# Token sums in spare operand tiles, and a feed-forward block whose down product runs beside its gate and up pairs

## The chip, the cores and the metric

One core of one Trainium2 chip runs the whole program in one launch. The metric is the device time of one execution in microseconds (us). Engines: PE (TensorE) multiplies, DVE (VectorE), ACT (ScalarE) and POOL (GpSimd) work elementwise, SP issues the loads.

## The reference, cut to what matters

Two blocks of two layers each work on x with 512 tokens and 1024 features. The change touches the feed-forward parts only:

```python
# first block, each layer
h = rms_norm(x, mlp_norm_w)
x = x + jnp.square(jax.nn.relu(h @ w_up)) @ w_down        # 4096 hidden features
# second block, each layer
def swiglu(h, w_gate, w_up, w_down):
    return (jax.nn.silu(h @ w_gate) * (h @ w_up)) @ w_down # 2816 hidden features
h = rmsnorm(x, ffn_pre_g[layer])
x = x + rmsnorm(swiglu(h, ffn_w_gate[layer], ffn_w_up[layer], ffn_w_down[layer]), ffn_post_g[layer])
```

The norms divide each token by its root mean square; the kernel applies that factor (`rb`, spread over partitions; `rT`, one column per block of 128 tokens) after the products, and only the per-feature weights before them.

## The kernel before, in words

All matrices lie with features on the partitions, so that a tile of 128 output features by 512 tokens is the sum of k products of a 128x128 weight block with a 128x512 input block. Every fp32 operand is split into a high part (fp32r, an ACT copy) and a low part (the difference, by DVE or POOL), and each block product is three matmuls: high by high, high by low, low by high (`mm3`, L318). `weights` (L260) loads one tile of weights into `raw` (4 buffers), and makes `whi` and `wlo` (3 buffers each). `fm_tiles` (L329) makes plain tiles: 8 blocks of inputs by 3 matmuls of 512 columns.

Most gate, up and hidden tiles are made in pairs by `seven` (L402), a Strassen-like scheme: seven half-size products (each 4 blocks by 3 matmuls of 256 columns, 84 matmuls in all) give two output tiles. It needs sums of weight quarters (`pair_weights`, L374: four POOL additions at L393 to L397 into two `sum` tiles, then an ACT copy to `shi` at L386 and a DVE subtraction to `slo` at L387) and sums of token halves (`token_sums`, L352, once for each feed-forward part: eight scaled ACT copies into the temporaries b1 and b2, sixteen DVE subtractions into four `sum` tiles one after the other, an ACT copy and a DVE subtraction into `tok`). `sum` has 2 buffers, which the token sums and the weight sums of the pairs share; b1 has 1 buffer and b2 is one of the four temporaries `t`. `shi` and `slo` have 3 buffers in the first block and 2 in the second.

`seven` is a generator with three steps: products 1 to 3 (p1 with the weight half a1, p2 and p3 with s12), then the second half of p1 and p2 with s34, then the last two (p2 with a2, p3 with s34) and `post`. In `mlp` (L948) and `swiglu` (L1344) `pairs` runs the first two steps of a pair and leaves the third to come after the first step of the next one (`finish`). The weight sums are issued in the first step.

In `mlp` four hidden tiles are plain (`up`), and after every 8 hidden tiles the down product of that group follows: 8 output tiles in a row (`down`, L971).

In `swiglu` tiles 0, 1 and 21 are plain (gate and up each), tiles 2 to 20 are 19 pairs. `post` multiplies gate and up by `rb` (L1364, L1365), takes silu on ACT (L1350) and the product on DVE (L1351), and splits the result: high part on ACT (L275), low part on POOL (L276). The hidden tiles fall into groups of 6, 6, 6 and 4; after each group its down product makes 8 output tiles in a row, copied to `m` by ACT for the first group (L1386) and added by DVE for the others (L1389). So five pairs stand in a row, then eight down tiles, and so on. `act`, the operand tiles of the hidden features, has 10 buffers in `mlp` and 8 in `swiglu`. `post_norm` (L1054) then norms `m` and adds it to x.

The order on each engine is made by the framework's planner from its own estimates of time, with the program's order as priority: an instruction written later can stand earlier on its engine. Each engine then works its list strictly in that order.

Of the kernel before, what the change touches and what calls it, by code (L numbers as in the profile page):

```python
# [8 lines left out]
F = mybir.dt.float32  # L9
R = mybir.dt.float32r  # L10
# [69 lines left out]
def host_arrays(inp):  # L80
# [69 lines left out]
    dn = g["ffn_w_down_2"]  # L150
    out["down012"] = np.stack([np.stack([fm(dn[l][768 * i:768 * i + 768]) for i in range(3)]) for l in range(2)])
    out["down3"] = np.stack([fm(dn[l][2304:]) for l in range(2)])
    out["odin"] = fm(g["od_w_in_2"][0])
# [7 lines left out]
class Net:  # L161
# [189 lines left out]

    def token_sums(self, x, g):  # L352


        nc, out, high = self.nc, [], self.last_high
        for k in range(4):
            b1, b2 = self.temp("b1", 1), self.temp()
            for i, b in enumerate((b1, b2)):
                nc.scalar.activation(b, x[k + 4 * i], AF.Copy, scale=g(k + 4 * i))
            (b11, b12), (b21, b22) = [(b[:, :256], b[:, 256:]) for b in (b1, b2)]  # L360
            f = self.get("sum", 2 * S)
            t1, t2, t3, t4 = [f[:, 256 * i:256 * i + 256] for i in range(4)]
# [39 lines left out]
    def seven(self, src, xg, tok, post):  # L402
# [18 lines left out]
        r, t, u = self.get("r", 256), self.temp(), self.temp()  # L421
        product(p1, a1, 0, plain(0, 0), True)
        product(p2, s12, 1, summed(1), True)
        product(p3, s12, 0, summed(0), True)
# [7 lines left out]
        nc.vector.tensor_add(u[:, half[1]], p3, u[:, half[1]])  # L432
        yield
        product(p2, a2, 0, summed(3), False)
        product(p3, s34, 1, plain(1, 1), False)
        nc.vector.tensor_add(u[:, half[0]], p2, r)
        nc.vector.tensor_add(t[:, half[1]], p3, t[:, half[1]])
        post(t, u)
# [59 lines left out]

    def mean_sq(self, accs, dim, eps=EPS, warm=False):


        nc = self.nc
        ps = self.av_tile()
        for i, acc in enumerate(accs):
            for tb in range(NB):
                self.stat_mm = nc.tensor.matmul(
                    ps[:, 2 * tb:2 * tb + 2], acc[:, tb * 128:(tb + 1) * 128], self.ones2,
                    start=i == 0 and tb == 0, stop=i == len(accs) - 1, skip_group_check=True)
            if warm:
                self.keep_warm(7, self.stat_mm)  # L510
        var = self.small(4, "var")
        nc.vector.tensor_scalar(var, ps[:, 0:8:2], 1.0 / dim, eps, op0=OP.mult, op1=OP.add)
        return var
# [434 lines left out]
    def mlp(self, l):  # L948
        nc, I, x = self.nc, self.I, self.x
        xg, _, rb = self.pre_norm("mlp_norm", l)  # L950
        acts = {}

# [24 lines left out]
        def pairs(js):  # L977
            for j in js:
                now = both(j)
                next(now)  # L980
                finish()
                next(now)
                left.append(now)

# [5 lines left out]
        up([3])  # L990
        tok = self.token_sums(x, lambda c: self.v("mlp_norm", 8 * l + c))
        pairs([4, 6])
# [60 lines left out]

    def post_norm(self, m, name, l, then, last=False):  # L1054

        nc = self.nc
        accs = self.sumsq(m, apart=True)
        rb = self.spread_psum(self.rsqrt(self.mean_sq(accs, 1024, warm=not last)))
        if not last:
# [17 lines left out]

    def post_pre_norm(self, m, post, pl, pre, l):
        xg = []

        def then(c):
            xg.append(self.split_scaled(self.x[c], self.v(pre, 8 * l + c), self.normed()))
            return self.last_low

        self.post_norm(m, post, pl, then)
        return (xg,) + self.rstd(self.sumsq(self.x, apart=True, eng=self.nc.gpsimd), 1024)
# [257 lines left out]
    def swiglu(self, l):  # L1344
        nc, I = self.nc, self.I
        xg, rT, rb = self.normed_x
        acts, m, left = {}, [], []

        def product(j, t, u):
            nc.scalar.activation(t, t, AF.Silu)  # L1350
            nc.vector.tensor_mul(t, t, u)  # L1351
            acts[j] = self.split(t, nc.gpsimd)

        def tile(ps):
            t = self.temp()
            nc.vector.tensor_mul(t, ps, rb)
            return t
# [4 lines left out]
        def both(j):  # L1362
            def post(t, u):
                nc.vector.tensor_mul(t, t, rb)  # L1364
                nc.vector.tensor_mul(u, u, rb)  # L1365
                product(j, t, u)
            return self.seven([I[n][l, j] for n in ("gate", "up")], xg, tok, post)

        def pairs(js):
            for j in js:  # L1370
                now = both(j)
                next(now)
                finish()
                next(now)
                left.append(now)

        def finish():
            while left:
                next(left.pop())

        def down(g, n, j):
            src = I["down012"][l, g, j] if g < 3 else I["down3"][l, j]
            ps = self.fm_tile(self.weights(src, n * 128, nc.vector), [acts[6 * g + k] for k in range(n)])
            if g == 0:
                t = self.get("m", S)
                nc.scalar.activation(t, ps, AF.Copy)  # L1386
                m.append(t)
            else:
                nc.vector.tensor_add(m[j], m[j], ps)  # L1389

        p = self.fm_tiles([plain("gate", 0), plain("up", 0), plain("gate", 1)], xg)
        last = self.fm_tiles([plain("up", 1)], xg)[0]
        tok = self.token_sums(self.x, lambda c: self.v("ffn_pre", 8 * l + c))
        product(0, tile(p[0]), tile(p[1]))
        product(1, tile(p[2]), tile(last))
        pairs(range(2, 6))
        for g, n in enumerate((6, 6, 6, 4)):
            if g < 3:
                pairs([6 * g + 6])
            down(g, n, 0)  # L1400
            finish()
            for j in range(1, 8):
                down(g, n, j)
            if g < 2:
                pairs(range(6 * g + 7, 6 * g + 12))
            elif g == 2:
                pairs([19, 20])
                t = tile(self.fm_tile(plain("gate", 21)[0], xg))
                finish()
                product(21, t, tile(self.fm_tile(plain("up", 21)[0], xg)))  # L1410
        if l == 0:
            self.normed_x = self.post_pre_norm(m, "ffn_post", 0, "mix_pre", 1)
        else:
            self.post_norm(m, "ffn_post", 1, self.store, last=True)

# [24 lines left out]
```

## Time and profile before

| what | value |
|---|---|
| three runs | 2532.81, 2529.24, 2529.79 us, median 2529.79 |
| the profiled execution | 2529.73 us, its span from first to last instruction 2528.0 us |
| PE busy | 2359.3 us (93%), DVE 1736.7 (69%), ACT 1216.2 (48%), POOL 1019.9 (40%) |
| mean granted TensorE clock | 0.978 |
| feed-forward parts | about 310 to 660 and 997 to 1305 us (first block), 1531 to 1907 and 2117 to 2528 us (second block) |

The profile is one execution. Lines such as L387 are lines of the kernel before. A row of the timeline is an instruction's start, its duration, its engine and line, what it writes and reads, and in brackets the idle time of the engine before it with the work that ended it. A matmul's duration overlaps its neighbours; the distance from start to start is what a matmul costs.

### The profile page before, as it was taken

To read this page: it belongs to the slowest core of one execution; us is meant where nothing else is said; L and a number is where in the kernel's file an instruction comes from. 1 tells how busy PE (TensorE), PEld (TensorE's weight loads), DVE (VectorE), ACT (ScalarE), POOL (GpSimd) and SP (SyncE) were. 2 spreads that over 40 slices of the span, in tenths; PEclk is the share of its full clock that TensorE was granted. 3 is DMA by queue.
4 is the path that set the end of the run, shared out by engine and by line. 5 is a ranking of instruction groups with operands and counts; after the bars stand their busy time and mean duration, and the time that the engine had idled before them with its cause. 6 is when DMAs were issued, how large, how long until landed. Compare 5 with 4: busy or idle time off the path is not lost.

```text
span 2528.0 us, 35109 instructions
## 1 busy us (share of the span) xinstructions
PE 2359.3 (93%) x13521; PEld 2028.6 (80%) x13521; DVE 1736.7 (69%) x2777; ACT 1216.2 (48%) x1945; POOL 1019.9 (40%) x691
## 2 busy tenths in 40 slices
PE   9999979999998998999999997999999989799997
PEld 7787778898877876898887875888986766788886
DVE  6978664665488886565558668856857676857765
ACT  5657653443365675443343474443434554444432
POOL 3465343343145642444312432553521542634531
PEclk9999989999999999999999999999999999899998
DMA  5311223333232111333332211333222321233231
GB/s 171 100 63 44 65 76 100 105 104 93 90 101 83 58 51 59 107 94 100 101 100 72 84 43 42 100 101 100 83 91 71 102 79 56 74 102 93 94 102 59
DMA packets 63850, 215.71 MB, mean 85 GB/s; under 512 B 7105, under 2 KB 7233, under 8 KB 63681
## 3 DMA queue, kind: packets, MB, share of 16 engines
q1 hardware_dynamic: 62064, 207.06, 26.9%
q0 software_dynamic: 1472, 6.29, 0.7%
q8 instruction: 106, 1.74, 0.3%
q14 instruction: 64, 0.52, 0.1%
q10 hardware_dynamic: 144, 0.11, 0.0%
HBM read 211.33 MB, written 2.10 MB: 84 GB/s over the span
## 4 chain that ended last, share of the span: by engine, by line
PE 69%; DVE 20%; ACT 4%; issue 4%; POOL 2%; DMA 0%; POOLq 0%; ACTq 0%; DVEq 0%
PE mm L323 19%; PE mm L322 19%; PE mm L321 19%; PE st L322 2%; PE st L321 2%; DVE wlo L387 2%; PE st L323 2%; DVE slo L387 1%; DVE x L1065 1%; DVE t L1365 1%; PE st L307 1%; DVE score L737 1%; DVE m L736 1%; PE st L308 1%; PE st L632 1%
## 5 line engine op out<-in xcount | busy, mean ns | idle before, releaser
L268 ACT ACTIVATE whi<-raw 128x1024 fp32r<-128x1024 f32 (+2 forms) x286 | 277.7, 973 | 488.5 <-PE mm L322 310.2
L321 PE MATMUL mm<-xg,whi 128*128 128x512 f32 (+1 forms) x1280 | 446.7, 355 | 31.0 <-ACT r L425 17.1
L321 PE MATMUL mm<-act,whi 128*128 128x512 f32 x1160 | 456.2, 396 | 10.3 <-ACT act L275 8.3
L322 PE MATMUL mm<-act,whi 128*128 128x512 f32 x1160 | 460.3, 397 | 0.8 <-POOL act L276 0.8
L323 PE MATMUL mm<-act,wlo 128*128 128x512 f32 x1160 | 460.3, 398 | 0.0
L323 PE MATMUL mm<-xg,wlo 128*128 128x512 f32 (+1 forms) x1280 | 453.0, 355 | 3.4 <-DVE wlo L269 2.4
L322 PE MATMUL mm<-xg,whi 128*128 128x512 f32 (+1 forms) x1280 | 453.6, 355 | 0.2
L269 POOL TENSOR_TENSOR wlo<-raw,whi 128x1024 fp32r<-128x1024 f32 (+3 forms) x109 | 257.8, 2367 | 295.3 <-ACT whi L268 285.0
L321 PEld LDWEIGHTS mm<-xg,whi 128*128 128x128 f32 x1280 | 244.4, 192 | 71.2 <-ACT xg L314 19.9
L276 POOL TENSOR_TENSOR act<-t,act 128x512 fp32r<-128x512 f32 x108 | 145.2, 1355 | 387.6 <-ACT act L275 387.6
L387 DVE TENSOR_TENSOR slo<-sum,shi 128x1024 fp32r<-128x1024 f32 x128 | 172.7, 1349 | 185.6 <-ACT shi L386 185.2
L322 PEld LDWEIGHTS mm<-xg,whi 128*128 128x128 f32 x1280 | 244.9, 191 | 37.7 <-DVE xg L315 6.6
L323 PEld LDWEIGHTS mm<-xg,wlo 128*128 128x128 f32 x1280 | 244.6, 191 | 37.2 <-DVE wlo L269 4.9
L321 PEld LDWEIGHTS mm<-act,whi 128*128 128x128 f32 x1160 | 220.6, 191 | 62.8 <-ACT act L275 11.1
L322 PEld LDWEIGHTS mm<-act,whi 128*128 128x128 f32 x1160 | 218.6, 188 | 52.6 <-DVE act L276 2.3
L386 ACT ACTIVATE shi<-sum 128x1024 fp32r<-128x1024 f32 x128 | 135.8, 1061 | 256.1 <-POOL sum L394 119.1
L323 PEld LDWEIGHTS mm<-act,wlo 128*128 128x128 f32 x1160 | 218.4, 188 | 47.7
L269 DVE TENSOR_TENSOR wlo<-raw,whi 128x1024 fp32r<-128x1024 f32 (+3 forms) x177 | 200.2, 1131 | 68.5 <-ACT whi L268 67.8
L393 POOL TENSOR_TENSOR sum<-raw 128x512 f32<-128x512 f32 x64 | 96.7, 1510 | 310.8 <-DMA raw<-in_w1up 129.5
L387 DVE TENSOR_TENSOR wlo<-raw,whi 128x1024 fp32r<-128x1024 f32 (+1 forms) x128 | 179.2, 1403 | 14.9 <-ACT whi L386 13.1
L321 PE MATMUL mm<-tok,shi 128*128 128x256 f32 x512 | 147.9, 289 | 33.8 <-ACT shi L386 29.5
L323 PE MATMUL mm<-tok,slo 128*128 128x256 f32 x512 | 149.1, 291 | 29.2 <-DVE slo L387 29.2
(276 smaller groups left out, 5196.0 us busy)
## 6 DMA issues: line engine op xcount, KB each, us to landing
raw<-in_w1up SPq DMA_DIRECT2D x64, 512.0 KB, 3.6
raw<-in_w1down SPq DMA_DIRECT2D x64, 512.0 KB, 3.6
raw<-in_gate SPq DMA_DIRECT2D x44, 512.0 KB, 3.6
raw<-in_up SPq DMA_DIRECT2D x44, 512.0 KB, 3.6
raw<-in_w1fm SPq DMA_DIRECT2D x41, 512.0 KB, 3.5
raw<-in_down SPq DMA_DIRECT2D x48, 384.0 KB, 3.0
raw<-in_odin SPq DMA_DIRECT2D x16, 512.0 KB, 3.6
raw<-in_w1out SPq DMA_DIRECT2D x16, 384.0 KB, 3.0
```

The lines of the kernel that those rows point to most:

```text
L268: self.last_high = nc.scalar.activation(hi[:, sl], raw[:, sl], AF.Copy)
L269: (low or nc.gpsimd).tensor_sub(lo[:, sl], raw[:, sl], hi[:, sl].bitcast(F))
L276: (low or nc.vector).tensor_sub(lo, t, hi.bitcast(F))
L307: mm(ps, a[:, rows], b[hh][:, cols], start=True, stop=False, skip_group_check=True)
L308: self.last_mm = mm(ps, a[:, rows], lo[hh][:, cols], start=False, stop=last, skip_group_check=True)
L321: mm(ps, w[0], a[0], start=first, stop=False, skip_group_check=True)
L322: mm(ps, w[0], a[1], start=False, stop=False, skip_group_check=True)
L323: self.last_mm = mm(ps, w[1], a[0], start=False, stop=last, skip_group_check=True)
L386: nc.scalar.activation(hi[:, :width], t, AF.Copy)
L387: nc.vector.tensor_sub(lo[:, :width], t, hi[:, :width].bitcast(F))
L393: nc.gpsimd.tensor_add(s1, a21, a22)
L632: nc.tensor.transpose(tr[:, o:o + 128], pr[:, QOFF[qb] + sb * 128:QOFF[qb] + sb * 128 + 128], self.ident)
```

## The change

Three edits. First, both feed-forward parts take six `act` tiles before any hidden tile needs them (`spare`), and the token sums use these: four for the sums, two for the scaled copies. They no longer touch `sum`, b1 or the temporaries. Second, `seven` gets one more step (it stops after p1 alone), and its last two products change places; `mlp` calls one step more. Third, `swiglu` works in groups of 2, 4, 4, 4, 4 and 4 hidden tiles, tiles 2 to 21 are now 20 pairs, and beside each pair stand two tiles of the former group's down product, one before and one after the pair's last step. The low part of a hidden tile moves from POOL to DVE, `u` is no longer multiplied by `rb`, and `post_norm` makes up for that factor with small operations on 128x4 tiles.

```diff
-    out["down012"] = np.stack([np.stack([fm(dn[l][768 * i:768 * i + 768]) for i in range(3)]) for l in range(2)])
-    out["down3"] = np.stack([fm(dn[l][2304:]) for l in range(2)])
+    out["down2"] = np.stack([fm(dn[l][:256]) for l in range(2)])
+    out["down4"] = np.stack([np.stack([fm(dn[l][512 * i - 256:512 * i + 256]) for i in range(1, 6)]) for l in range(2)])
...
-    def token_sums(self, x, g):
+    def spare(self, n):
+        return [self.get("act", 2 * S, R).bitcast(F) for _ in range(n)]
+
+    def token_sums(self, x, g, spare):
...
         for k in range(4):
-            b1, b2 = self.temp("b1", 1), self.temp()
+            b = spare[4 + k % 2]
+            b1, b2 = b[:, :S], b[:, S:]
...
-            f = self.get("sum", 2 * S)
+            f = spare[k]
...
         product(p1, a1, 0, plain(0, 0), True)
+        yield
         product(p2, s12, 1, summed(1), True)
...
         yield
+        product(p3, s34, 1, plain(1, 1), False)
         product(p2, a2, 0, summed(3), False)
-        product(p3, s34, 1, plain(1, 1), False)
+        nc.vector.tensor_add(t[:, half[1]], p3, t[:, half[1]])
         nc.vector.tensor_add(u[:, half[0]], p2, r)
-        nc.vector.tensor_add(t[:, half[1]], p3, t[:, half[1]])
...
+        if scale is not None:
+            square = self.small(4, "square")
+            nc.vector.tensor_mul(square, scale, scale)
...
+            nc.vector.scalar_tensor_tensor(var, ps[:, 0:8:2], 1.0 / dim, square, op0=OP.mult, op1=OP.mult)
+            nc.vector.tensor_scalar(var, var, eps, None, op0=OP.add)
...
     def mlp(self, l):
...
-        acts = {}
+        acts, spare = {}, self.spare(6)
...
                 next(now)
                 finish()
                 next(now)
+                next(now)
                 left.append(now)
...
-        rb = self.spread_psum(self.rsqrt(self.mean_sq(accs, 1024, warm=not last)))
+        r = self.rsqrt(self.mean_sq(accs, 1024, warm=not last, scale=scale))
+        if scale is not None:
+            nc.vector.tensor_mul(r, r, scale)
+        rb = self.spread_psum(r)
...
     def swiglu(self, l):
...
-            acts[j] = self.split(t, nc.gpsimd)
+            acts[j] = self.split(t)
...
                 nc.vector.tensor_mul(t, t, rb)
-                nc.vector.tensor_mul(u, u, rb)
                 product(j, t, u)
...
+        def down(g, js):
+            src = I["down4"][l, g - 1] if g else I["down2"][l]
+            first, n = (4 * g - 2, 4) if g else (0, 2)
+            ws = [(self.weights(src[j], n * 128, nc.vector), 0) for j in js]
+            for j, ps in zip(js, self.fm_tiles(ws, [acts[first + k] for k in range(n)])):
+                if g == 0:
+                    t = self.get("m", S)
+                    nc.scalar.activation(t, ps, AF.Copy)
+                    m.append(t)
+                else:
+                    nc.vector.tensor_add(m[j], m[j], ps)
+
+        p = self.fm_tiles([plain("gate", 0), plain("up", 0), plain("gate", 1)], xg)
+        p += self.fm_tiles([plain("up", 1)], xg)
+        tok = self.token_sums(self.x, lambda c: self.v("ffn_pre", 8 * l + c), spare)
+        for j in range(2):
+            product(j, scaled(p[2 * j]), p[2 * j + 1])
+        for j in range(2, 22):
+            g, i = divmod(j - 2, 4)
+            now = both(j)
+            for _ in range(3):
                 next(now)
...
+            down(g, [2 * i])
+            next(now)
+            down(g, [2 * i + 1])
+        down(5, range(3))
+        for j in range(3, 8):
+            down(5, [j])
```

Both `post_norm` calls of `swiglu` get `rT` as `scale`. The loops over groups of 6, the function `tile` for `u` and the plain products of tile 21 are gone.

## Rows read from the trace of the kernel before

**Rows 1.** Stretches: from:to, us, busy of PE, PEld, DVE, ACT, POOL, clock, DMA.

```profile
365.00:655.00 290.00, 289.51 (x1724) 256.94 (x1723) 162.97 (x201) 119.44 (x164) 102.58 (x75) 1.00 0.33 99
...
1600.00:1642.00 42.00, 38.30 (x290) 36.72 (x291) 34.44 (x46) 19.09 (x29) 18.72 (x12) 1.00 0.30 92
1642.00:1680.00 38.00, 38.00 (x210) 32.91 (x209) 14.02 (x16) 15.28 (x23) 15.55 (x11) 1.00 0.40 120
1682.00:1694.00 12.00, 11.16 (x93) 10.95 (x93) 10.93 (x13) 6.48 (x9) 8.04 (x5) 1.00 0.29 80
```

**Rows 2.** Groups on PE, 1594 to 1900 and 2180 to 2470: busy, mean ns | idle before.

```profile
L323 PE MATMUL mm<-tok,slo 128*128 128x256 f32 x140 | 40.7, 291 | 13.9 <-DVE slo L387 13.9
...
L323 PE MATMUL mm<-tok,slo 128*128 128x256 f32 x136 | 39.6, 291 | 13.8 <-DVE slo L387 13.8
```

**Rows 3.** Timeline of PE: one pair of the second block, and a down tile.

```profile
1600.89 0.39 PE L323 MATMUL mm<-tok,slo 128*128 128x256 f32 x1 [0.93 <-DVE slo L387]
...
1610.90 0.28 PE L322 MATMUL mm<-tok,shi 128*128 128x256 f32 x1
1612.59 0.39 PE L323 MATMUL mm<-tok,slo 128*128 128x256 f32 x1 [1.40 <-DVE slo L387]
...
1642.10 0.40 PE L322 MATMUL mm<-act,whi 128*128 128x512 f32 x1
...
1644.88 0.40 PE L322 MATMUL mm<-act,whi 128*128 128x512 f32 x1
```

**Rows 4.** Timelines of DVE and POOL in that pair, and of DVE later.

```profile
1606.89 2.20 DVE L387 TENSOR_TENSOR wlo<-raw,whi 128x1024 fp32r<-128x1024 f32 x1
...
1662.45 1.23 DVE L387 TENSOR_TENSOR wlo<-raw,whi 128x1024 fp32r<-128x1024 f32 x1
...
1607.96 2.28 POOL L397 TENSOR_TENSOR sum<-raw,sum 128x512 f32<-128x512 f32 x1
```

**Rows 5.** Stretches around the start of the pairs, columns as in Rows 1.

```profile
333.80:360.00 26.20, 13.63 (x75) 12.74 (x73) 19.92 (x26) 14.52 (x20) 14.56 (x11) 0.67 0.14 40
...
998.00:1022.00 24.00, 10.96 (x61) 10.29 (x60) 18.84 (x25) 13.01 (x20) 12.31 (x9) 0.64 0.15 43
...
1565.40:1588.00 22.60, 9.66 (x61) 9.25 (x60) 18.21 (x18) 10.17 (x14) 15.87 (x9) 0.70 0.16 47
2152.00:2174.00 22.00, 9.47 (x58) 9.06 (x57) 17.99 (x18) 9.56 (x14) 15.50 (x9) 0.69 0.16 48
```

**Rows 6.** Timelines of SP, POOL, PE: the pairs' start, first feed-forward part.

```profile
315.21 2.06 SPq L257 DMA_DIRECT2D raw<-in_w1up  x2
...
345.23 1.39 POOL L393 TENSOR_TENSOR sum<-raw 128x512 f32<-128x512 f32 x1 [6.77 <-DVE tok L370]
...
343.94 0.58 PE L321 MATMUL mm<-xg,whi 128*128 128x256 f32 x1 [8.54 <-ACT r L425]
```

**Rows 7.** Timelines of SP, POOL, PE: the pairs' start, third feed-forward part.

```profile
1522.12 0.33 SPq L257 DMA_DIRECT2D raw<-in_up  x1
...
1571.56 2.18 POOL L393 TENSOR_TENSOR sum<-raw 128x512 f32<-128x512 f32 x1 [1.16 <-DVE tok L370]
...
1577.08 0.58 PE L321 MATMUL mm<-tok,shi 128*128 128x256 f32 x1 [11.29 <-ACT shi L386]
```

**Rows 8.** The page: loads, KB each, median us from issue to landing.

```profile
raw<-in_up SPq DMA_DIRECT2D x44, 512.0 KB, 3.6
```

**Rows 9.** Groups by shape, whole span: count | busy us, mean ns | idle before.

```profile
L370 DVE TENSOR_TENSOR tok<-sum,tok 128x1024 fp32r<-128x1024 f32 x16 | 21.6, 1357 | 2.4 <-ACT tok L369 2.2
...
L1365 DVE TENSOR_TENSOR t<-t,rb 128x512 f32<-128x512 f32 x38 | 42.8, 1126 | 0.3
L1389 DVE TENSOR_TENSOR m<-m,mm 128x512 f32<-128x512 f32 x48 | 33.0, 687 | 58.4 <-PE mm L323 58.3
...
L276 DVE TENSOR_TENSOR act<-o,act 128x512 fp32r<-128x512 f32 x16 | 11.0, 686 | 6.0 <-ACT act L275 6.0
L540 DVE TENSOR_TENSOR part<-rest,part 128x4 bf16<-128x4 f32 x15 | 2.4, 161 | 0.3
```

More of the change, by code (lines that the diff above doesn't have):

```diff
@@ L497, in sumsq, with mean_sq @@
         return accs
-    def mean_sq(self, accs, dim, eps=EPS, warm=False):
+    def mean_sq(self, accs, dim, eps=EPS, warm=False, scale=None):
         nc = self.nc
+        if scale is not None:
+            square = self.small(4, "square")
+            nc.vector.tensor_mul(square, scale, scale)
         ps = self.av_tile()
@@ L511, in mean_sq @@
         var = self.small(4, "var")
-        nc.vector.tensor_scalar(var, ps[:, 0:8:2], 1.0 / dim, eps, op0=OP.mult, op1=OP.add)
+        if scale is None:
+            nc.vector.tensor_scalar(var, ps[:, 0:8:2], 1.0 / dim, eps, op0=OP.mult, op1=OP.add)
+        else:
+            nc.vector.scalar_tensor_tensor(var, ps[:, 0:8:2], 1.0 / dim, square, op0=OP.mult, op1=OP.mult)
+            nc.vector.tensor_scalar(var, var, eps, None, op0=OP.add)
         return var
@@ L990, in mlp @@
         up([3])
-        tok = self.token_sums(x, lambda c: self.v("mlp_norm", 8 * l + c))
+        tok = self.token_sums(x, lambda c: self.v("mlp_norm", 8 * l + c), spare)
         pairs([4, 6])
@@ L1052, in final_norm, with post_norm @@
         return xg, rT, rb, normed
-    def post_norm(self, m, name, l, then, last=False):
+    def post_norm(self, m, name, l, then, last=False, scale=None):
         nc = self.nc
         accs = self.sumsq(m, apart=True)
-        rb = self.spread_psum(self.rsqrt(self.mean_sq(accs, 1024, warm=not last)))
+        r = self.rsqrt(self.mean_sq(accs, 1024, warm=not last, scale=scale))
+        if scale is not None:
+            nc.vector.tensor_mul(r, r, scale)
+        rb = self.spread_psum(r)
         if not last:
@@ L1076, in pre_norm, with post_pre_norm @@
         return (xg,) + self.rstd(self.sumsq(self.x), 1024)
-    def post_pre_norm(self, m, post, pl, pre, l):
+    def post_pre_norm(self, m, post, pl, pre, l, scale=None):
         xg = []
@@ L1083, in then @@
             return self.last_low
-        self.post_norm(m, post, pl, then)
+        self.post_norm(m, post, pl, then, scale=scale)
         return (xg,) + self.rstd(self.sumsq(self.x, apart=True, eng=self.nc.gpsimd), 1024)
@@ L1346, in swiglu @@
         xg, rT, rb = self.normed_x
-        acts, m, left = {}, [], []
+        acts, m, spare = {}, [], self.spare(6)
         def product(j, t, u):
@@ L1351, in product, with scaled @@
             nc.vector.tensor_mul(t, t, u)
-            acts[j] = self.split(t, nc.gpsimd)
-        def tile(ps):
+            acts[j] = self.split(t)
+        def scaled(ps):
             t = self.temp()
@@ L1364, in post @@
                 nc.vector.tensor_mul(t, t, rb)
-                nc.vector.tensor_mul(u, u, rb)
                 product(j, t, u)
             return self.seven([I[n][l, j] for n in ("gate", "up")], xg, tok, post)
-        def pairs(js):
-            for j in js:
-                now = both(j)
-                next(now)
[L1373 to L1410, printed above, removed]
+        def down(g, js):
[7 more added lines that the diff above has]
+                    m.append(t)
+                else:
+                    nc.vector.tensor_add(m[j], m[j], ps)
@@ L1411, in swiglu @@
+        down(5, range(3))
+        for j in range(3, 8):
+            down(5, [j])
         if l == 0:
-            self.normed_x = self.post_pre_norm(m, "ffn_post", 0, "mix_pre", 1)
+            self.normed_x = self.post_pre_norm(m, "ffn_post", 0, "mix_pre", 1, rT)
         else:
-            self.post_norm(m, "ffn_post", 1, self.store, last=True)
+            self.post_norm(m, "ffn_post", 1, self.store, last=True, scale=rT)
 @with_exitstack
```

## The prediction

> **What bounds the kernel now.** I read the busy shares first (the table above): PE is busy 93% of the span, so PE's work and PE's waits make the time, and other engines count only where PE waits for them. Then I read stretches. In the first block, once its pairs are under way, PE is busy for 289.5 of 290 us at the full clock of 2.4 GHz: nothing to win there. In the second block five pairs in a row leave it 38.3 of 42 us, the down tiles that follow 38.0 of 38.0, and DVE is busy for 10.93 of 12 us while pairs run, for 14.0 of 38 while down tiles run [rows 1]. So there the limit alternates, DVE for pairs and PE for down tiles. The groups on PE name the wait: p2 with s34 waits for its low part `slo`, 13.9 and 13.8 us of idle time in the two feed-forward parts of that block [rows 2]. In the timeline one pair lasts 1612.59 - 1600.89 = 11.70 us, of which 83 steps from start to start take 10.01 us (0.1206 each), and then PE stands until `slo` comes [rows 3]. Last I read the start of the pairs, where the waits are long: 8.54 us in the first block, 11.29 in the second, with the mean granted clock at 0.64 to 0.70 [rows 5 to 7].
>
> **The sum** is made against the profiled execution, 2529.73 us (span 2528.0, and 1.7 around it); the median of the runs is 2529.79, so no correction.
>
> **1. Pairs of the second block.** PE's work for a pair is 84 x 0.1206 = 10.1 us, so 1.6 us of 11.70 is lost; by start to start that is 1.57 / 1.40 times the idle time of its row [rows 3], so 27.7 us of idle time [rows 2] are worth 31. Afterwards two down tiles stand beside each pair: 12 matmuls of 512 columns take 1644.88 - 1642.10 = 2.78 us [rows 3], so PE needs 10.1 + 5.6 = 15.7 us for a step (12.9 for the first four, whose down tiles have half the blocks). DVE now spends 10.93 x 11.70 / 12 = 10.7 us on a pair [rows 1]. It loses the multiplication of u (1.13), and gains the low part of the hidden tile (0.69) and, for each down tile, a 512-column low part (0.69 again) and the addition to `m` (0.69) [rows 9]: 10.7 - 1.13 + 0.69 + 2.76 = 13.0 us against 15.7 of PE (about 11.1 against 12.9 in the first four, whose eviction is ACT's). DVE is no longer the limit, so the wait should go. It is not quite all: the lists are strict, and some head-of-line waiting stays. Ends: 0 to 31 us. I take 28, near the upper end, since in the first block pairs beside a DVE that is busy for 163 of 290 us wait for nothing [rows 1]. What is late next is a1's high and low part: its buffer comes free with a down tile (a rival, below).
>
> **2. Tile 21 as half a pair.** The plain products of 48 matmuls of 512 columns cost 4 x 2.78 = 11.1 us, a pair 10.1: 1 us less in each part, **2** in all, on PE's path.
>
> **3. Start of the pairs.** At the lost clock and the waits together: 26.2 us for 75 matmuls that need 75 x 0.1206 = 9.0, then 24.0 for 61, 22.6 for 61 and 22.0 for 58 [rows 5]: lost are 17.2 + 16.6 + 15.2 + 15.0 = 64 us. In the first block the two loads issued from 315.21 on complete the raw weights of the first pair, landed by about 318.9 at 3.6 us each, but POOL's first sum waits until 345.23, for the DVE subtraction of a token sum that holds a `sum` buffer [rows 6, 8]. In the second the last load for the first pair is issued at 1522.12, landed at 1525.7, and its sums wait until 1571.56 for the same thing [rows 7, 8]. With tiles of their own the token sums release POOL by 26 and 46 us, far more than the wait; what is late next is `tok` itself. It costs DVE four low parts of 1.36 us [rows 9] and sixteen half-width subtractions, on ACT twelve copies. In the first block x is ready before the four plain tiles, whose 96 matmuls take PE 8 x 2.78 = 22 us [rows 3], and b1, the one buffer that made the copies take turns, is gone: time enough for all of `tok`, and I keep 3 of 17 us. In the second the plain tiles run while the norm's chain still holds DVE, chunk by chunk, so less of that time is free and I keep about 5 of 15. Gain: 14 + 14 + 10 + 10 = **48**. Ends: 0 (tok was the real bound) and 64.
>
> **4. Priced at little.** `post_norm` gets three operations on 128x4 tiles, two of them in the chain at the end of each part: 4 x 0.16 = **0.6** us longer in all [rows 9]. The low part leaves POOL and costs DVE the 0.69 counted above. The down loads are smaller and twice as many in number per column, 16 issues more in each part, on SP, which has nothing else there; behind them wait the next pair's loads, covered by a step of 15.7 us against 3.6 us to landing [rows 8]. The last group keeps its size; its first three tiles run together, against 0 to 1 us for the third one's weights, and the wait for the last hidden tile there now has a down tile before it; I put these at 0. The new order of the last two products, and the earlier `finish` in `mlp`, have no wait to remove where PE is at 289.5 of 290 [rows 1]; ends: +3 to -1 us in all, taken as 0.
>
> Sum: -28 - 2 - 48 + 0.6 = -77; 2529.7 - 77 = **2453 us**.
>
> **A rule weighed against a row.** A DVE subtraction of 1024 columns takes 2.20 us beside POOL's sum and 1.23 later: 0.97 us for one POOL instruction, which itself takes 2.28 there and 1.39 elsewhere [rows 4, 6]. So each POOL sum moved beside DVE work that is on the path costs up to 0.97. The Trainium skill, SBUF — State Buffer, section Who interferes with whom, says that the port pair of the two is an exclusive lock, held for a whole instruction. By it the price would be the full length of the other's instruction; this trace shows less.
>
> **The rivals.**
> - *The token operands bind.* `tok` is made on DVE and ACT as before; for it: DVE is busy for 19.9 of 26.2 and 18.2 of 22.6 us in these stretches [rows 5]. Against it: in both POOL's sums, not `tok`, came last [rows 6, 7]. Then half of part 3 is won: 2453 + 24 = 2477.
> - *The sums fall on the norm.* POOL's sums, free of the tokens, run in the second block beside the norm's DVE chain, before which they were held. Four sums at the full 1.39 us each delay it by 5.6 us in each of two parts (at 0.97: 3.9) and the rest of the gain holds: 2453 + 11 = 2464. The lock of the page SBUF — State Buffer (the Trainium skill) would act so.
> - *The wait moves to a1.* Four tiles of weights share three `whi` buffers in a step. If a1 of the next pair is late by 1 us in each of 40 steps: 2453 + 40 - 3 = 2490.
> - *Slower.* The same buffers, worse: if a1's buffer comes free only with the second down tile, its DVE subtraction (1.23 to 2.20) [rows 4] and before it an ACT copy of the same size, which I estimate at the lower of these, stand on PE's path at every step, less what p1's first matmuls cover: some 2.6 us x 40 = 104: 2529.7 + 104 - 31 - 2 - 48 + 0.6 = 2553. It decides from 80 / 40 = 2.0 us a step. Against it: a1's buffer can be the first down tile's, free 5.7 us (2.78 + 24 x 0.1206) before it is needed.
> - *It does not do what it says.* The planner leaves POOL's sums behind the tokens, and only parts 1 and 2 come: 2453 + 48 = 2501.
>
> **How the numbers follow.** Forecast 0.58; tokens bind 0.15; sums on the norm 0.12; a1 late 0.06; slower 0.04; order unchanged 0.05. All waits of parts 1 and 3 gone would give 2529.7 - 31 - 2 - 64 = 2433. I give 2436 to 2486, which holds the first three cases and leaves out the last three, 0.15, and a little at the low end. A measurement of this kernel can tell about 0.2%, 5 us, from no change. Faster 0.95, same 0.01, slower 0.04.
>
> **What would show it.** Right: POOL's first sum of a part no longer ended by a tok subtraction; the wait of p2 at the start under 6 us and the granted clock of these stretches above 0.85; in the second block the `slo` wait of PE under 3 us in all, and steps of 15.7 us from p1 to p1; DVE below 90% there. Wrong: PE idle at p1 waiting for `whi` or `wlo` (a1 late), steps of more than 17 us (slower), p2 waiting for `tok` for over 6 us, or a longer chain of the norm on DVE.

## The result and the profile after

| | median of the runs | range | profiled execution |
|---|---|---|---|
| before | 2531.30 us (4 runs) | 2529.24 to 2533.80 | 2529.73 |
| after | 2573.16 us (4 runs) | 2568.10 to 2577.51 | 2568.10, span 2566.3 |

The ratio is 1.0164, with a 95% interval of 1.0143 to 1.0186: slower by 1.6%, where 3% faster was forecast. Between the profiled executions, of which the one after is the fastest of its four, it is 38.4 us.

**Where it went.** The norms mark the stages. On PE each has a first `av<-ones,acc` matmul (sum of squares) and a first `av<-identb,part` matmul (spreading the factor). The timeline of PE before, at such marks of the first feed-forward part (two lines) and the third (three):

```profile
320.55 0.39 PE L506 MATMUL av<-ones,acc 128*128 128x2 f32 x3
...
676.64 0.39 PE L506 MATMUL av<-ones,acc 128*128 128x2 f32 x3
...
1525.21 0.39 PE L506 MATMUL av<-ones,acc 128*128 128x2 f32 x3
...
1557.83 0.34 PE L543 MATMUL av<-identb,part 128*128 128x128 bf16 x3
...
1923.08 0.35 PE L506 MATMUL av<-ones,acc 128*128 128x2 f32 x2
```

and the same after:

```profile
321.38 0.35 PE L515 MATMUL av<-ones,acc 128*128 128x2 f32 x2 [0.50 <-DVE acc L502]
...
684.04 0.28 PE L515 MATMUL av<-ones,acc 128*128 128x2 f32 x2
...
1542.88 0.28 PE L515 MATMUL av<-ones,acc 128*128 128x2 f32 x2
...
1579.54 0.44 PE L556 MATMUL av<-identb,part 128*128 128x128 bf16 x2
...
1950.43 0.35 PE L515 MATMUL av<-ones,acc 128*128 128x2 f32 x2
```

The first part takes 684.04 - 321.38 = 362.7 us against 356.1, the norms ahead of the third 36.7 against 32.6, the third 370.9 against 365.2. Read in this way, in us of one profiled execution each (rows below "after" are the experiments; code that is the same in two kernels differs by up to 3 us in these columns):

| kernel | first block, part 1 | part 2 | norms | second block, part 1 | norms | part 2 |
|---|---|---|---|---|---|---|
| before | 356.1 | 356.1 | 32.6 | 365.2 | 32.6 | 364.8 |
| after | 362.7 | 366.0 | 36.7 | 370.9 | 36.0 | 372.3 |
| e1_rawd2 | 360.2 | 364.9 | 37.6 | 340.6 | 37.6 | 340.9 |
| e2_p2_first | 360.5 | 360.1 | 36.2 | 349.5 | 36.3 | 349.1 |
| e3_old_tokens | 367.9 | 370.5 | 32.6 | 373.6 | 32.6 | 375.6 |
| e4_old_swiglu | 364.3 | 364.6 | 37.5 | 379.0 | 35.6 | 381.2 |
| e5_both | 358.6 | 358.9 | 38.0 | 338.5 | 36.0 | 339.6 |
| e6_finish_later | 351.3 | 353.0 | 36.3 | 338.6 | 36.1 | 339.6 |
| e7_spare_only | 353.0 | 353.7 | 37.7 | 359.3 | 36.2 | 359.0 |
| e8_norm_first | 351.1 | 353.0 | 33.6 | 344.4 | 33.7 | 343.9 |
| e9_tokens_first | 352.5 | 352.9 | 36.8 | 341.7 | 36.2 | 338.8 |
| e10_both_first | 352.2 | 352.6 | 36.3 | 340.3 | 35.6 | 339.1 |
| e11_low_on_pool | 351.4 | 353.3 | 36.8 | 341.8 | 36.9 | 340.7 |
| e12_hidden_low_on_pool | 351.2 | 353.1 | 36.0 | 339.0 | 36.4 | 339.5 |

So after the change all six stages are longer: 16.5 us in the first block, 7.5 in the norms, 13.2 in the second block.

**The start of the pairs** did get shorter. The stretches of [rows 5], shifted by each part's delay:

```profile
334.90:361.10 26.20, 15.33 (x99) 14.54 (x98) 20.14 (x25) 15.32 (x24) 13.67 (x10) 0.74 0.17 60
1006.20:1030.20 24.00, 13.75 (x84) 13.25 (x83) 19.07 (x24) 13.55 (x21) 12.97 (x9) 0.79 0.16 54
1587.10:1609.70 22.60, 17.51 (x115) 16.02 (x114) 16.96 (x25) 13.85 (x22) 6.08 (x4) 0.92 0.23 63
2183.10:2205.10 22.00, 17.81 (x112) 16.73 (x113) 17.68 (x24) 13.51 (x21) 6.10 (x4) 0.84 0.22 66
```

PE does 24, 23, 54 and 54 matmuls more in them than before; at 0.1206 us each that is, as an estimate, 18.7 us won, not 48, and the norms give 7.5 of it back.

In the first block PE now waits for `tok`, 5.60 us at 350.15. Part of that wait looks to be POOL's doing: the four subtractions ahead of the first `tok` copy take 1.51, 1.30, 1.48 and 1.48 us while POOL works beside them; the next four of the same shape take 0.41 to 0.42 with POOL idle. The fourth of each, and POOL beside the first of the two:

```profile
347.53 1.48 DVE L371 TENSOR_TENSOR act<-act,act 128x256 f32<-128x256 f32 x1
...
350.05 0.42 DVE L371 TENSOR_TENSOR act<-act,act 128x256 f32<-128x256 f32 x1
...
347.29 1.44 POOL L276 TENSOR_TENSOR act<-t,act 128x512 fp32r<-128x512 f32 x1
```

That is 4.1 us of DVE's time; no run tried how much shorter the wait is without it.

**In the second block** the page shows the `slo` wait of PE gone, and a new wait on POOL:

```profile
L398 POOL TENSOR_TENSOR sum<-raw 128x512 f32<-128x512 f32 x66 | 86.8, 1315 | 670.2 <-DMA raw<-in_up 262.5
...
L323 PE MATMUL mm<-tok,slo 128*128 128x256 f32 x528 | 150.0, 284 | 0.4 <-DVE slo L392 0.4
```

On PE p3 with s34 waits in its place, for DVE's addition at L438 (1594 to 1940 us):

```profile
L321 PE MATMUL st<-xg,shi 128*128 128x256 f32 x80 | 24.9, 311 | 22.4 <-DVE t L438 22.4
```

POOL's first weight sum waits for the load of the up weights. The timelines of one step (SP, POOL, ACT, DVE, then PE at the first matmul of p3 with s34) show a closed loop:

```profile
1742.26 0.33 SPq L257 DMA_DIRECT2D raw<-in_up  x1
...
1746.04 1.29 POOL L398 TENSOR_TENSOR sum<-raw 128x512 f32<-128x512 f32 x1 [11.88 <-DVE t L432]
...
1748.53 1.30 POOL L399 TENSOR_TENSOR sum<-sum,raw 128x512 f32<-128x512 f32 x1
...
1749.86 1.06 ACT L391 ACTIVATE shi<-sum 128x1024 fp32r<-128x1024 f32 x1 [5.41 <-POOL sum L399]
...
1750.96 1.33 DVE L392 TENSOR_TENSOR slo<-sum,shi 128x1024 fp32r<-128x1024 f32 x1 [4.95 <-ACT shi L391]
...
1753.26 0.42 DVE L438 TENSOR_TENSOR t<-st,t 128x256 f32<-128x256 f32 x1
...
1753.74 0.39 PE L321 MATMUL st<-xg,shi 128*128 128x256 f32 x1 [1.18 <-DVE t L438]
...
1756.76 0.63 ACT L391 ACTIVATE whi<-raw 128x512 fp32r<-128x512 f32 x1 [0.29 <-PE mm L322]
...
1759.29 0.33 SPq L257 DMA_DIRECT2D raw<-in_up  x1
...
1770.84 0.39 PE L321 MATMUL st<-xg,shi 128*128 128x256 f32 x1 [1.27 <-DVE t L438]
```

The load lands 3.6 us after its issue, at 1745.9 (in 10 of 16 such steps the trace names it as what the first sum waited for; in the others, as here, DVE's `t`, L432, ended within 0.1 us of it). Three sums, of which `shi` needs the first and the third, then `shi` and `slo` of the next pair follow. Behind `slo` in DVE's list stand the current pair's evictions (`t`, L437 and L438); p3 waits for the last of them, p2 with a2 stands behind p3; then a2's copy of the next pair can be made, its low part, and only this frees the raw buffer of the next load. The distance is 1759.29 - 1742.26 = 17.03 us, the same as 1770.84 - 1753.74 = 17.10 at p3, within 0.1. PE needs 15.7.

**In the first block** p3 waits too, but at the starts of groups and not at every step. DVE before such a wait, and PE:

```profile
442.40 2.17 DVE L392 TENSOR_TENSOR slo<-sum,shi 128x1024 fp32r<-128x1024 f32 x1
444.49 1.75 DVE L392 TENSOR_TENSOR wlo<-raw,whi 128x512 fp32r<-128x512 f32 x1
...
446.61 0.42 DVE L438 TENSOR_TENSOR t<-st,t 128x256 f32<-128x256 f32 x1
...
447.09 0.39 PE L321 MATMUL st<-xg,shi 128*128 128x256 f32 x1 [2.81 <-DVE t L438]
```

Before the change 36 matmuls of the next pair stood between p2 with s34 and the products that need its eviction; now there are 12, over by 444.3, and DVE works through two low parts first. Beside POOL's work these take 2.17 and 1.75 us; in the steps of the second block operations of the same shapes take 1.23 and 0.69 (at 1756.49 and 1758.57). The group of p3 on PE (365 to 660 us) has 6.9 us of idle time, and as much in the second part:

```profile
L321 PE MATMUL st<-xg,shi 128*128 128x256 f32 x52 | 15.3, 293 | 6.9 <-DVE t L438 6.9
```

### The profile page after: what moved, and what is told of

The parts are those of the page before. It is cut to its first block, busy times and chain, and to the rows that moved or that the text cites. A ratio compares the mean times of both kernels' runs of the same rounds, so it can differ in the third digit from the quotient of the medians.

```text
span 2566.3 us, 35401 instructions
## 1 busy us (share of the span) xinstructions
PE 2380.7 (93%) x13593; PEld 2038.3 (79%) x13593; DVE 1721.4 (67%) x2861; ACT 1223.0 (48%) x1985; POOL 924.9 (36%) x655
## 4 chain that ended last, share of the span: by engine, by line
PE 54%; DVE 21%; issue 8%; ACT 7%; POOL 6%; DMA 4%; POOLq 0%; SPq 0%; ACTq 0%; DVEq 0%
PE mm L321 14%; PE mm L322 14%; PE mm L323 14%; DMA raw<-in_up 4%; ACT shi L391 3%; PE st L321 2%; PE st L322 2%; PE st L323 2%; POOL sum L401 2%; POOL sum L399 2%; POOL sum L398 2%; DVE x L1083 1%; DVE wlo L392 1%; DVE wlo L269 1%; DVE score L750 1%
## 5 line engine op out<-in xcount | busy, mean ns | idle before, releaser
L268 ACT ACTIVATE whi<-raw 128x1024 fp32r<-128x1024 f32 (+3 forms) x314 | 279.2, 891 | 451.4 <-PE mm L322 279.0
L321 PE MATMUL mm<-xg,whi 128*128 128x512 f32 (+1 forms) x1264 | 441.0, 355 | 35.6 <-ACT whi L391 12.2
L323 PE MATMUL mm<-xg,wlo 128*128 128x512 f32 (+1 forms) x1264 | 447.1, 354 | 3.7 <-DVE wlo L392 2.3
L322 PE MATMUL mm<-xg,whi 128*128 128x512 f32 (+1 forms) x1264 | 447.7, 354 | 0.2
L398 POOL TENSOR_TENSOR sum<-raw 128x512 f32<-128x512 f32 x66 | 86.8, 1315 | 670.2 <-DMA raw<-in_up 262.5
L276 POOL TENSOR_TENSOR act<-t,act 128x512 fp32r<-128x512 f32 x64 | 101.3, 1598 | 188.4 <-ACT act L275 180.0
L321 PE MATMUL mm<-tok,shi 128*128 128x256 f32 x528 | 151.5, 287 | 12.2 <-ACT tok L374 11.2
L322 PE MATMUL mm<-tok,shi 128*128 128x256 f32 x528 | 149.7, 284 | 0.0
```

Of the source, the lines that this page charges most:

```text
L268: self.last_high = nc.scalar.activation(hi[:, sl], raw[:, sl], AF.Copy)
L276: (low or nc.vector).tensor_sub(lo, t, hi.bitcast(F))
L321: mm(ps, w[0], a[0], start=first, stop=False, skip_group_check=True)
L322: mm(ps, w[0], a[1], start=False, stop=False, skip_group_check=True)
L323: self.last_mm = mm(ps, w[1], a[0], start=False, stop=last, skip_group_check=True)
L398: nc.gpsimd.tensor_add(s1, a21, a22)
```

## The experiments

**Own raw buffers for the down tiles** (room for them comes from one `r` buffer less and from a zero tile at the start that shares another's memory):

```diff
+        if own:
+            raw = self.get("rawd", width)
...
-            ws = [(self.weights(src[j], n * 128, nc.vector), 0) for j in js]
+            ws = [(self.weights(src[j], n * 128, nc.vector, True), 0) for j in js]
...
-        with self.phase(act=8, m=8, tok=4, sum=2, shi=2, slo=2, r=2):
+        with self.phase(act=8, m=8, tok=4, sum=2, shi=2, slo=2, r=1, rawd=2):
```

> The changed kernel, with two raw buffers of 512 columns for the down tiles of the feed-forward alone, so that the four common raw buffers serve the pairs only (room for them: one r buffer instead of two there). Theory (loop): the step of 17.03 us is a closed loop through the raw buffers: the load of the next pair's up weights waits for the low part of a2, then come three POOL sums, shi, slo, and behind slo on DVE the evictions that p3 and p2 with a2 wait for. With buffers to spare the load is issued a step earlier, POOL's sums start 3 to 8 us earlier, and a step falls to PE's 15.7 to 16.0 us: 2 x 17 x 1.2 = 41 us, total 2525 to 2540. Rival (order): DVE's list and PE's order of products set the step whatever the loads do: steps of 16.8 to 17.1, total 2565 to 2577. Rival (rivalry of ports or load time): POOL's sums start earlier but each takes longer beside DVE, steps of 16.3 to 16.7, total 2545 to 2560.

Measured: 2505.39 us, ratio to before 0.9892 (0.9870 to 0.9915); below the range that the loop gave, by 20 us. The timelines of SP and POOL; and then a stretch of three steps, columns as in [rows 1]:

```profile
1728.58 0.33 SPq L261 DMA_DIRECT2D raw<-in_up  x1
...
1733.57 1.62 POOL L402 TENSOR_TENSOR sum<-raw 128x512 f32<-128x512 f32 x1 [5.57 <-DVE slo L396]
...
1744.17 0.33 SPq L261 DMA_DIRECT2D raw<-in_up  x1
```

```profile
1691.00:1738.50 47.50, 47.50 (x333) 44.45 (x332) 38.34 (x49) 20.66 (x31) 17.74 (x12) 1.00 0.32 100
```

A step is 15.59 us, PE is never idle in this stretch, and POOL's sum waits for a `sum` buffer and no longer for the load. The parts of the second block fall by 30.3 and 31.4 us; 20 steps at 17.03 - 15.59 = 1.44 us are 29, where the theory had counted 17 at 1.2. The loop through the raw buffers is shown; DVE, now busy for 38 of 47.5 us, was not the limit.

**p2 with a2 first:**

```diff
-        product(p3, s34, 1, plain(1, 1), False)
         product(p2, a2, 0, summed(3), False)
-        nc.vector.tensor_add(t[:, half[1]], p3, t[:, half[1]])
+        product(p3, s34, 1, plain(1, 1), False)
         nc.vector.tensor_add(u[:, half[0]], p2, r)
+        nc.vector.tensor_add(t[:, half[1]], p3, t[:, half[1]])
```

> The changed kernel with the last two products of a pair in the old order: p2 with a2 before p3 with s34, and their two additions likewise; the extra step and all else stay. Theory (loop): a2's buffer comes free up to 1.9 us earlier in a step, since p2 then doesn't stand behind p3's wait for the second addition to u; the loop of 17.03 us shortens to 15.7 to 16.2, and the 2.9 us waits at the group boundaries of the first block (p3 behind p2 with s34) fall to under 1.5: total 2525 to 2550. Rival (slo late, whatever the order): POOL's sums come when the load lands, slo behind them, and the wait moves to p2, steps 16.8 to 17.1, total 2562 to 2575.

Measured: 2516.90 us, ratio 0.9934 (0.9911 to 0.9956). The second block's parts fall by 21.4 and 23.2 us. A stretch of three steps, and the group of POOL's first sum (1640 to 1900 us):

```profile
1700.00:1747.00 47.00, 47.00 (x326) 43.60 (x325) 31.02 (x48) 18.83 (x29) 13.93 (x11) 1.00 0.31 101
```

```profile
L398 POOL TENSOR_TENSOR sum<-raw 128x512 f32<-128x512 f32 x15 | 20.1, 1339 | 156.0 <-DMA raw<-in_up 94.0 <-DVE act L276 52.5 <-DVE wlo L269 9.4
```

For most of its idle time the sum still waits for the load, and yet PE is busy for 47.0 of 47.0 us: the loop is cut at its other place. The 8 to 9 us a part by which this run stays behind the one with own raw buffers are, in the first, lost in the main ahead of this stretch (PE is busy for 43.0 of 50 us from 1600 to 1650, there for 48.6). In the first block the gain is 2.2 and 5.9 us; waits of 1.9 and 2.2 us remain at the group starts, now of p2 for the first eviction, where under 1.5 was expected.

**The token sums as before** (four `sum` buffers in turn, `b1` and a temporary; the diff of the change, undone):

> The changed kernel with the token sums as before: four sum buffers in turn, b1 and a temporary for the scaled copies, no spare operand tiles. Theory: the early POOL sums of the first pair brought nothing, since tok itself comes as late as before, and in the second block they delay the norm by 3.4 to 4.0 us in each part; so without them the time is 2560 to 2575, and the starts of the pairs look as they did before. Rival: the spare tiles are worth the 48 us that were forecast, and the loss is elsewhere: 2600 to 2620.

Measured: 2578.68 us, ratio 1.0181 (1.0164 to 1.0199). The norms return to 32.6 us, a gain of 4.1 and 3.4; the first block loses 5.2 and 4.5, the second 2.7 and 3.3. The median lies 4 us above the range expected: in the first block the spare tiles do earn something. They do not earn 48.

**The second block as before,** with the spare tiles and the changed order in a pair kept (`swiglu` and the down weights undone):

> The changed kernel with the second block's feed-forward as before (groups of 6, tile 21 plain, low part on POOL, u multiplied by rb, norm without the extra factor), but with the spare tiles for the tokens and the changed order in a pair. Theory: the first block keeps its loss of 16 us, the norms their 7.4, and the second block falls back to its steps of before, with or without their wait for slo: 2545 to 2560. Rival (the new order in a pair is what costs, in both blocks): 2560 to 2580. Rival (the new grouping is worth 28 us as forecast): 2585 to 2605.

Measured: 2582.54 us, ratio 1.0185 (1.0159 to 1.0211): 2.5 us above the range of the first rival, which is the nearest, and my theory missed. The old grouping costs more with the new order (379.0 and 381.2 us, in an execution that is the slowest of its four, 2593.37) than with the old one. Its largest wait on PE, 1600 to 1900 us, is p3's:

```profile
L321 PE MATMUL st<-xg,shi 128*128 128x256 f32 x68 | 22.9, 337 | 25.3 <-DVE t L438 25.3
```

**Both edits,** own raw buffers and p2 first:

> The two former edits together: own raw buffers for the down tiles, and p2 with a2 before p3 with s34. Theory: the two cut the same loop of the second block at two places, so there they don't add up (each feed-forward part near 340 us, as with the raw buffers alone); in the first block p2 first saves 2 and 6 us, as it did alone: 2490 to 2500. Rival (the losses of the second block are two separate ones, 30 and 22 us a part): 2460 to 2480, which PE's own work of 329.4 us a part forbids below some 2485. Rival (with loads early, p2 first brings the wait on a2's weights back): 2500 to 2510.

Measured: 2496.00 us, ratio 0.9873 (0.9853 to 0.9892). As expected they don't add up in the second block (338.5 and 339.6 us), since they cut one loop.

**Finish later,** on top of both:

```diff
                 next(now)
-                finish()
                 next(now)
+                finish()
                 next(now)
                 left.append(now)
```

> As the run with both edits, and in the first block the last step of a pair comes after the whole first step of the next one again (p1, p2, p3, then finish), as before the change. Theory: in the first block the extra step left only p1 (12 matmuls, 1.4 us) between p2 with s34 and the products that need its eviction, where 36 matmuls (4.3 us) stood before; the waits of 1 to 3 us at the starts of groups and the clock lost behind them go, a part falls from 353 to 344 to 347 us, total 12 to 18 below the run with both edits. Rival (the token sums in spare tiles are what costs in the first block): within 4 us of it.

Measured: 2479.78 us, ratio 0.9804 (0.9787 to 0.9820). The first block falls by 7.3 and 5.9 us, and past its first pairs PE waits for no eviction any more; a stretch of its first part after the change and here, columns as in [rows 1]:

```profile
365.00:660.00 295.00, 288.08 (x1699) 254.47 (x1698) 162.83 (x199) 116.67 (x161) 103.46 (x74) 0.99 0.31 97
365.00:660.00 295.00, 295.00 (x1746) 261.90 (x1745) 165.37 (x207) 121.73 (x167) 100.16 (x74) 1.00 0.32 100
```

With the swap, the order in a pair had cost the first block 362.7 - 351.3 = 11.4 and 13.0 us.

**Spare tiles alone,** in the kernel before:

> The kernel before with the token sums in spare tiles, and nothing else of the change. Theory: the first block gains about 5 us a part, as the changed kernel lost that much when its spare tiles were taken away; in the second the start gains 3 us and the norm ahead of it loses 4: total 2518 to 2526. Rival (forecast): the sums of the first pair came last, so 40 to 50 us less: 2480 to 2490. Rival (no effect, tok binds alone): 2529 to 2534.

Measured: 2524.32 us, ratio 0.9973 (0.9964 to 0.9983), so 0.2% to 0.4%. First block -3.1 and -2.4 us, norms +5.1 and +3.6, second block -5.9 and -5.8.

**The norm first:** POOL's first weight sum of a part is ordered behind the norm's power.

```diff
+        first = nc.gpsimd.tensor_add(s1, a21, a22)
+        if self.norm_first:
+            self.after(first, self.last_rstd)
```

> As the run with finish later, and in the second block POOL's first weight sum of each part stands behind the power (rstd) of the norm on POOL. Theory (sums fall on the norm): DVE's chain of the norm, no longer beside POOL's sums, is 3 to 4 us shorter in each part, and the sums are still early enough for tok: 6 to 8 us less than that run. Rival (the first pair is late by as much): within 2 us of it. Rival (the sums, now between norm and tok, cost more than they did): 2 to 8 us more.

Measured: 2483.12 us, ratio 0.9827 (0.9807 to 0.9846), 3.3 us more than the run without it, though the two intervals overlap. The norms get 2.7 and 2.4 us shorter, but the parts behind them get 5.8 and 4.3 us longer. The end of the norm's chain with the sums beside it (finish later; DVE, then POOL):

```profile
1548.78 1.77 DVE L1087 TENSOR_TENSOR x<-x,m 128x512 f32<-128x512 f32 x1
1550.47 1.75 DVE L506 TENSOR_TENSOR acc<-acc,t 128x512 f32<-128x512 f32 x1
1552.15 1.75 DVE L319 SCALAR_TENSOR_TENSOR xg<-x,vec_sb,xg 128x512 fp32r<-128x512 f32 x1
...
1548.27 1.73 POOL L405 TENSOR_TENSOR sum<-raw,raw 128x512 f32<-128x512 f32 x1
1549.96 1.71 POOL L403 TENSOR_TENSOR sum<-sum,raw 128x512 f32<-128x512 f32 x1
```

and without them (the norm first):

```profile
1546.28 0.69 DVE L1091 TENSOR_TENSOR x<-x,m 128x512 f32<-128x512 f32 x1
1546.88 0.69 DVE L510 TENSOR_TENSOR acc<-acc,t 128x512 f32<-128x512 f32 x1
1547.76 0.75 DVE L320 SCALAR_TENSOR_TENSOR xg<-x,vec_sb,xg 128x512 fp32r<-128x512 f32 x1 [0.19 <-ACT xg L319]
...
1551.50 1.27 POOL L403 TENSOR_TENSOR sum<-raw 128x512 f32<-128x512 f32 x1
1552.73 1.26 POOL L409 TENSOR_TENSOR sum<-raw,raw 128x512 f32<-128x512 f32 x1
```

The three DVE operations take 1.08 + 1.06 + 1.00 = 3.1 us more beside POOL's sums. That is most of the norm's loss of 3.4 to 5.1 us. What the early sums are worth to the pairs this run doesn't tell, since the later sums fall on the norm as well, on its last small operations: three of 128x4 (at 1551.56, 1554.19 and 1555.52) take 1.22 to 1.23 us each beside them, against 0.16 to 0.17 in finish later. All but the first of these stand in the parts' 5.8 and 4.3 us.

**The tokens first:** in the first block the call of `token_sums` stands ahead of the four plain tiles.

> As the run with finish later, and in the first block the token sums are written ahead of the four plain tiles instead of behind them (same instructions, same spare tiles). Theory (the tokens bind, by their place in the program): the eight scaled copies, which stand on ACT behind the fourth plain tile's high part though x and the tiles are there 25 us earlier, come from 312 us on; tok is there when the plain tiles end, the two waits of PE at the start (4.9 and 5.6 us in each part) fall to under 3 together, and with the clock a part is 7 to 12 us shorter: 2456 to 2466. Rival (the token sums then fall on the norm's DVE chain, which runs at the same time): the norm is later by 4 to 6 us and half is given back: 2467 to 2474. Rival (the spare tiles themselves come free late, or another wait stands behind): within 3 us of that run.

Measured: 2476.54 us, ratio 0.9785 (0.9763 to 0.9808), which overlaps that of the run with finish later. The copies do come early, and the wait for `tok` goes, but a plain tile now waits for its low part, which DVE makes among the tokens (ACT, DVE, PE):

```profile
310.97 0.71 ACT L368 ACTIVATE act<-x,vec_sb 128x512 f32<-128x512 f32 x1
...
326.66 2.35 DVE L379 TENSOR_TENSOR tok<-act,tok 128x1024 fp32r<-128x1024 f32 x2
...
326.80 0.79 PE L327 MATMUL mm<-xg,wlo 128*128 128x512 f32 x1 [7.01 <-DVE wlo L273]
```

The wait has moved ahead of the pairs: DVE's work for `tok`, not its place alone, is what the start costs. So the theory missed (2456 to 2466 if the place were all), the case with another wait behind comes nearest, and of the gain of 3 us, which the intervals don't tell from none, not even that need come from the starts.

**The tokens first in both blocks:**

> As the run with the tokens first, in the second block too. There x comes chunk by chunk out of the norm before, whose chain holds DVE. Theory: the copies and subtractions move ahead of the plain tiles but between the norm's own operations, so the norm ends 3 to 6 us later and the start of the pairs 3 to 6 us earlier: within 4 us of the run with the tokens first in the first block alone. Rival (as good there as in the first block): 8 to 16 us less than that run.

Measured: 2478.21 us, ratio 0.9793 (0.9777 to 0.9809): no different, as expected.

**Low parts of the plain tiles on POOL,** in the first block, with the token sums between the third and the fourth:

> As the run with finish later; in the first block the token sums stand between the third and the fourth plain tile, and the low parts of the first three plain tiles' weights are made by POOL instead of DVE. Theory (DVE's time ahead of the pairs is the bound, 15 us for tok plus 1.2 for each low part): DVE is freed of 3.7 us, tok comes that much earlier, and no plain tile waits behind tok, as the third one did for 7.0 us in the run with the tokens first: a part 2 to 5 us shorter than in the run with finish later, 2470 to 2476. Rival (POOL's low parts, 2.3 to 2.6 us each, come late for the plain tiles and hold back the pairs' sums): 2480 to 2490.

Measured: 2495.25 us, ratio 0.9860 (0.9844 to 0.9877), 5 us above the range of the rival, and the theory missed. The wait that costs is one that the rival did not name: PE waits 5.25 us for the norm's sums on DVE (0.46 in finish later):

```profile
326.87 0.34 PE L519 MATMUL av<-ones,acc 128*128 128x2 f32 x1 [5.25 <-DVE acc L506]
```

DVE makes these sums beside POOL's low parts and weight sums: the last six take 7.52 us in all from 319.20, where one takes 0.68 in the run with the tokens first. The feed-forward parts themselves are as long as in finish later. The first block's start and the stage between its parts account for some 8 of the 14.0 us between the two profiled executions; the rest lies in stages whose code is the same.

**The hidden tiles' low part on POOL again,** in the second block, on top of finish later:

> As the run with finish later, with the low part of the second block's hidden tiles on POOL again, as before the change. Theory (DVE is not the limit of a step once the loads are early): within 4 us of that run. Rival (POOL becomes the step's limit or delays the sums and with them slo): each of 40 steps 0.3 to 0.6 us longer, 2492 to 2504. Rival (DVE still binds): 5 to 12 us less.

Measured: 2478.05 us, ratio 0.9790 (0.9771 to 0.9808): within 2 us, so that edit is worth nothing that these runs can tell.

## Why the prediction was wrong

**The order of the last products and the earlier `finish`** (step 4: "have no wait to remove", +3 to -1 us) is the step that failed worst. I looked only for a wait to remove and not for one that it adds. That PE was busy for 289.5 of 290 us [rows 1] says that every eviction was covered, not that its cover could be cut from 36 matmuls to 12 in the first block, or that p2 with a2 could be put behind p3's wait. It cost the first block 24.4 us (after against finish later). In the second, with the old grouping, it costs 19.7 and 22.2 (second block as before against spare tiles alone, which differ in the order and the extra step only); in all 58 us between the medians of those two kernels.

**Pairs of the second block** (step 1, -28). Right: the `slo` wait went, from 27.7 us [rows 2] to 0.4 (though p3's waits of 22.4 and 23.2 us came in its place), DVE has time left, and a step is 15.6 us once nothing else holds it. Wrong: "the wait should go", and that a1 is late next. I compared DVE's busy time with PE's, 13.0 to 15.7, and did not follow the chain that decides when `slo` can start: a load, its buffer, and who frees it. With four weight tiles a step for four raw buffers, the load of the next pair hung on the low part of a2, and so on p3. I had priced the 16 added loads of a part at nothing, "covered by a step of 15.7 us against 3.6 us to landing": the time to landing was right, the time of issue was the question. Raw buffers alone give back 62 us in the two parts.

**Size of steps 1 and 2 together,** once the loop is cut: from spare tiles alone to finish later the second block falls by 20.7 and 19.4 us, 40 against 30 forecast. The `slo` wait in the former is 13.9 and 13.0 us in the windows of [rows 2], 29.3 over the whole run, worth 33 by the prediction's factor of 1.57 / 1.40; the rest beyond step 2's single us a part I did not trace.

**Start of the pairs** (step 3, -48). Spare tiles alone measure -7 us. Right: POOL's sums were held by the tokens, and they came 26 us earlier in the first block, 319.40 for 345.23. Wrong: "time enough for all of `tok`". In the first block `tok` binds (PE waits 5.60 us for it at 350.15 after the change): its copies stand behind the fourth plain tile on ACT, when they are moved DVE has no room ahead of the pairs, and POOL's work beside the subtractions stretches them by 4.1 us. In the second POOL's sums fell on the norm: +4.1 and +3.4 us. Both were rivals in the text, at 0.15 and 0.12, and both came; the estimate of 3.9 us a norm came near (3.4 to 5.1), though partly by luck, as its 0.97 per sum was read from rows that show something else (last section). They should have been in the forecast.

**The slower rival** put its wait at a1's buffer, where none of this came; that the time lies beyond even its 2553 us has the other causes above.

**Together:** -7 (spare tiles) and -45 (grouping, with the order in a pair kept and the down loads in buffers of their own) give the 2479.8 us of finish later, 2% below the kernel before; the change as it was made loses 93 us of that to the order and the raw buffers. Part 2 was not tried by itself.

## What to carry to other kernels

An engine that is never idle has every wait covered by something: before an order is changed, count the work that stands between each producer and its consumer, and what the producer's engine has in its list ahead. When more tiles pass through a ring of buffers in a step, follow the ring once around, from issue to landing to the last reader to the next issue, and compare that length with the step; busy shares don't show it. Work released early runs beside whatever is there at that time, and should be charged for it.

## What the runs showed of the hardware

DVE and POOL almost take turns when both work on tiles of 512 columns. Beside each other they move in lockstep, one operation of each per 1.69 us (finish later: DVE from 1548.78 to 1550.47 to 1552.15, POOL from 1548.27 to 1549.96). Alone DVE's go from start to start in 0.60 (the norm first: 1546.28 to 1546.88), and POOL's in 1.25 (after the change: two such steps from 1746.04 to 1748.53, with DVE idle), 1.85 together. So 91% of strict turns, more than the prediction had taken from its rows.

It had read them wrongly: it set DVE's 2.20 us beside POOL's L397, which began 1.07 us later. Another POOL sum was under way when DVE began, in the kernel before:

```profile
1606.72 1.30 POOL L396 TENSOR_TENSOR sum<-raw,raw 128x512 f32<-128x512 f32 x1 [1.16 <-DVE slo L387]
```

DVE's subtraction began at 1606.89, when 1.13 us of that sum were left, and took 0.97 longer than elsewhere; L397 then took longer in its turn, while DVE ran on. So the 0.97 is most of what was left of a POOL instruction, and no upper bound: in the norm three operations lost 1.00 to 1.08. Even a cast of 4 columns, begun 0.06 us after a POOL sum in the norm first, took nearly the sum's whole time; in finish later, with POOL idle, it takes 0.17 (at 1556.25):

```profile
1551.56 1.23 DVE L558 CAST part<-rstd 128x4 bf16<-128x4 f32 x1 [1.13 <-POOL rstd L548]
```

The Trainium skill, SBUF — State Buffer, section Who interferes with whom, speaks of an exclusive lock on the port pair that the two share; "for the whole instruction" it says there of DVE's 2-port modes, and of a DVE instruction with two inputs in SBUF only that it contends with a POOL instruction that reads SBUF. Strict turns would be the 1.85 us, so this trace comes near to that rule, and the prediction, which took it for too strict, was the less right of the two.
